# A decoder layer in float32: block B22 loaded by the slot of its first sum, transposes ordered behind the matmuls in front of them

## The chip, the cores and the metric

One Trainium2 chip, of which the kernel uses one core. A core has TensorE (PE, with the weight load drawn apart as PEld), VectorE (DVE), ScalarE (ACT), GpSimd (POOL) and SyncE (SP), each with an instruction queue of its own, and 16 DMA engines that move data between HBM and on-chip memory (SBUF; matmuls write to PSUM). The metric is the device time of one execution in microseconds.

## The reference

One layer of a hybrid decoder on 256 tokens of width 2048, all in float32:

```python
h = rmsnorm(x, g_mix)
x_r, g_r, q, k, v, gate_r, gate_a = split(h @ w_in)
y_r = (gelu(g_r) * rg_lru(conv1d(x_r), ...)) @ w_rnn_out      # recurrent mixer
y_a = stick_breaking_attention(rmsnorm(q), rmsnorm(k), v) @ w_attn_out
x = x + (sigmoid(gate_r) * y_r + sigmoid(gate_a) * y_a) @ w_o
gate, up = split(rmsnorm(x, g_ffn) @ w_ffn_gu)
x = x + (silu(gate) * up) @ w_ffn_down
x = x + sigmoid(rmsnorm(x, g_ple) @ w_ple_gate) * (p @ w_ple_proj)
```

HBM reads are 405 MB, almost all weights, and nearly all of the work is products of 256 tokens with them.

## The kernel before, in words

**Numbers.** A float32 product is made of three matmuls in a reduced format (fp32r). Each weight block of 128 x 1024 numbers (512 KB) is loaded from HBM, ACT copies it to its high half `whi` (L363), DVE subtracts that to get the low half `wlo` (L364), and `prod` (L633) issues three matmuls: activations' high half with `whi` (L635), with `wlo` (L636), and the low half with `whi` (L637). A matmul of 512 columns is the unit of work.

**Fewer products.** From stage `ro` on, a product is cut in 2 x 2 blocks, and for some inner indices seven block products with sums of blocks take the place of eight. The weight blocks concerned are called 11, 12, 21 and 22; a slot called `T1` uses 11 + 12, `T2` uses that sum + 22, `T3` and `T4` are further ones, and `S1` to `S4` are the same for half blocks. These raw blocks come into tiles of the tag Q (31 of them). DVE adds them on chip (L288, in `summed`; for `T2` it is `add(t, t, r[g("22")])`, which therefore needs the block 22 landed), and some sums are made by POOL's transfers that add while they write (`joins`, L326). All other blocks go to `w` tiles, of which there are four (`W_BUFS`); a `w` tile is free again when DVE has made its `wlo`.

**Slots.** A group (`group`, the name with an index as in gu/2 or dn0/0) runs through a list of slots: `FIRST3`, `EVEN3`, `EVEN4`, `LONG` or `TWELVE`. In `EVEN4`, used by v and most of gu, the middle reads `... A2, B2, 10, "21", "T2", 11, "22", A3, 12 ...`: numbers are plain blocks, A and B the S sums. T2 comes ahead of 22, and 22 is needed from T2's addition on. The stages in order: gtr, the recurrent part, ro, v, attention, ao, wo, gu/0 to gu/3, dn0, gu/4 to gu/7, dn1, gu/8 to gu/10, dn2, pg.

**Order of the loads.** SyncE issues all loads of weights from one queue (L277), in an order written down ahead of time by `dma_order`. A list `t` of modelled times of the chunks gives each load a value `begin`; plain blocks by the use of the block whose buffer they take, raw blocks by `t` six chunks in front of their own slot, less `RAW_AHEAD`. `DMA_ORDER` sorts by `begin`. `dma_to` issues loads in this order, chained by `issue_after`, so a load behind one that waits for its buffer waits too. Splits run four chunks ahead of the matmuls in the program, and sums two more.

**Order of the rest.** A scheduler orders the instructions of each engine by its own modelled times when the kernel is built; `issue_after(x)` binds instructions built inside it to come behind x on the same engine. The engines run their queues in order, and semaphores make them wait for one another.

**Transposes.** Activations for the next stage are turned by TensorE against an identity (`next_mix` L1117, `turned` in `next_h` L1165, `turn` in `gu` L1226) and evacuated from PSUM by ACT (L449) and DVE (L443, L446). Such functions are put on the list `pend`; `group` takes one at the slots named in `TURNED_AT` (the fifth, seventh, ninth and eleventh in `FIRST3`, else the ninth to fifteenth). Element work goes on `todo` and is taken from the second slot on.

Of the kernel before, what the change touches and what calls it, by code (L numbers as in the profile page):

```python
# [42 lines left out]
FOUR = ("gu", "v")  # L43
LAST_GROUP = ("pg", 1)
W_BUFS = 4
RAW_AHEAD = 9.0
SUMS_AHEAD = 2
TURNED_AT = {True: (5, 7, 9, 11), False: (9, 11, 13, 15)}
NEG = -1e30
# [2 lines left out]
def pairs_of(name):  # L52

    if name[:2] == "dn":
        q = int(name[2])
        return [FQ0[q] // 2 + i for i in range(3 if FQ[q] == 16 else 2)]
    return (0, 1, 2, 3) if name in FOUR else (0, 1, 2)


def is_sum(x):  # L60

    return isinstance(x, str) or isinstance(x, tuple) and x[0] == "S"


def products(x, two=TWO):


    if isinstance(x, int):
        return [("2", (x, 0), None, 0), ("4", (x, 1), None, 0), ("3", (x, 0), None, 1), ("8", (x, 1), None, 1)]
    bank = {"11": "B", "T1": "5", "T2": "B", "T3": "B", "21": "2", "22": "3", "T4": "4"}  # L70
    if isinstance(x, str):
        return [(bank[x], x, p, c) for c, p in enumerate(two)]
    k = {1: ("11", "21"), 2: ("T1", "T2"), 3: ("22", "T3"), 4: ("T4",)}[x[1]]
    return [(bank[y], y, x[2], c) for c, y in enumerate(k)]
# [118 lines left out]
PLAN = plan()  # L193
# [9 lines left out]
CHUNKS = []  # L203
# [9 lines left out]
    LAST.append(len(CHUNKS))  # L213


def dma_order():


    t, took = [0.0], []
    for i, a, b in CHUNKS:  # L220
        k = PLAN[i][0]
        t.append(t[-1] + (0.68 * len(products(k[3])) if k[0] == "tok" and is_sum(k[3]) else 0.34 * (b - a)))
    plain, begin = [], {}
    for j, (i, _, _) in enumerate(CHUNKS):
        k = PLAN[i][0]
        if k[0] == "tok" and is_sum(k[3]):
            begin[j] = t[max(0, j - 6)] - RAW_AHEAD
        else:
            begin[j] = t[max(0, plain[-W_BUFS] - 4)] if len(plain) >= W_BUFS else 0.0
            plain.append(j)  # L230
    order = sorted(range(len(CHUNKS)), key=lambda j: begin[j])
    at = {j: n for n, j in enumerate(order)}
    upto, m = [0], 0
    for j in range(len(CHUNKS)):
        m = max(m, at[j] + 1)
        upto.append(m)
    return order, upto


DMA_ORDER, DMA_UPTO = dma_order()  # L240
HALVES = (1, 3)
CHUNK_OF = {PLAN[c[0]][0][1:]: j for j, c in enumerate(CHUNKS) if PLAN[c[0]][0][0] == "tok"}


class Stream:
# [37 lines left out]
    def summed(self, key):  # L283
# [33 lines left out]
        t = r[g("R")]  # L317
        self.dma_to(CHUNK_OF[g("22")] + 1)
        add(t, t, r[g("22")])
        return t, 1024  # L320

    def joins(self, t, c, key, a):

        j = CHUNK_OF[key]
        src = self.w[OFFS[j]:OFFS[j] + P * 1024].rearrange("(p c) -> p c", p=P)
# [90 lines left out]
def tile_hybrid_block(ctx: ExitStack, tc: tile.TileContext, xT: bass.AP, x: bass.AP, pT: bass.AP,  # L416
                      prm: bass.AP, w: bass.AP, out: bass.AP):
    nc = tc.nc
# [10 lines left out]
    def tl(tag, dt=F32):  # L429
        cnt[0] += 1  # L430
        tag = "H" if tag in "CT" else "Q"
        n, c = NT[tag]
        return act.tile([P, c], dt, tag=tag, name=f"{tag}_{cnt[0]}", bufs=n)

    def psum():
        cnt[0] += 1
        return pps.tile([P, 512], F32, tag="ps", name=f"ps_{cnt[0]}")
# [4 lines left out]
    def tt(o, a, b, op):  # L442
        nc.vector.tensor_tensor(o, a, b, op)  # L443
# [4 lines left out]
    def actv(o, i, f, **kw):  # L448
        nc.scalar.activation(o, i, f, **kw)  # L449
# [177 lines left out]
    pend, todo = [], []  # L627

    def tok(pairs, k, t):
        x = rhs(pairs, k)  # L630
        return x[:, t * P:t * P + P], x[:, 256 + t * P:384 + t * P]

    def prod(ps, x, wh, wl, start=False, stop=False, goes_on=False):  # L633

        nc.tensor.matmul(ps, x[0], wh, start=start, stop=False, skip_group_check=goes_on)  # L635
        nc.tensor.matmul(ps, x[0], wl, start=False, stop=False, skip_group_check=goes_on)  # L636
        nc.tensor.matmul(ps, x[1], wh, start=False, stop=stop, skip_group_check=goes_on)  # L637

    def half_sums(h):

# [58 lines left out]
    def group(at, pairs, sums, after=None, also=()):  # L699

        name, g = at
        slots = [x for n, y, _, _, _, sl in HEAD + TAIL if (n, y) == at for x in sl
                 if isinstance(x, int) or is_sum(x)]
        seq = [(n, q, 0, 512) for n, x in enumerate(slots) for q in products(x, pairs_of(name)[:2])]
        if at == LAST_GROUP:  # L710
            k = len(slots) - 4
            rest = [q for q in seq if q[0] >= k]
            seq = [q for q in seq if q[0] < k] + [q for b in "243" for q in rest if q[1][0] == b]
            seq += [(n, (b + f, *q), e, e + 256) for e, f in ((0, "a"), (256, "b")) for n, (b, *q), _, _ in rest
                    if b == "8"]
        first, last = {}, {}
        for i, (_, (b, y, _, _), e, _) in enumerate(seq):
            first.setdefault(b, i)
            last[b, e] = i
            if y in ("11", "T1", "T2", "T3"):  # L720
                last[y] = i
        banks, tile_, got = {}, {}, {}
        for i, (n, (b, y, p, c), e0, e1) in enumerate(seq):
            if n not in got:
                if n in also:
                    also[n]()
                if n and todo:
                    todo.pop(0)()
                elif n in TURNED_AT[slots[2] == 6 and slots[8] == "22"] and pend:
                    pend.pop(0)()  # L730
                got[n] = S_.take(("tok", name, g, slots[n]))
            if b not in banks:
                banks[b] = psum()
            ps = banks[b]
            if p is None:
                o = tok(pairs, *y)
            else:
                o = {"11": tok(pairs, 2 * p, 0), "21": tok(pairs, 2 * p + 1, 0), "22": sums[p][3],
                     "T1": sums[p][0], "T2": sums[p][1], "T3": sums[p][2],
                     "T4": tok(pairs, 2 * p + 1, 1)}[y]  # L740
            _, _, hi, lo, w0 = got[n].columns(c)
            s = slice(w0 + e0, w0 + e1)
            prod(ps[:, e0:e1], o, hi[:, s], lo[:, s], i == first[b], i in (last[b, e0], last.get(y)),
                 b == "B")
            if y in ("11", "T1", "T2", "T3") and i == last[y]:
                t = tile_[y] = tl("T")
                actv(t, ps, AF.Copy)
                if y == "T3":
                    tt(tile_["T2"], tile_["T1"], tile_["T2"], ALU.subtract)
                    tt(tile_["T1"], tile_["T1"], t, ALU.subtract)  # L750
                    if after is not None:
                        after(tile_)
        tile_["ends"] = [banks[b] for b in ("8a", "8b") if b in banks]
        return [banks[b] for b in "2438"], tile_


    xc, xcs, gel, y, gtr, ysum, xsum = {}, {}, {}, [], [], {}, {}
# [118 lines left out]
    for i in range(NPD):  # L876
        also.setdefault(2 * i + 1 if i < 7 else 14, []).append(squares_x(i))
    also = {n: (lambda fs: lambda: [f() for f in fs])(fs) for n, fs in also.items()}
    pss = group(("gtr", 0), xg, None, None, also)[0]
    qg = cst.tile([P, 1], F32, tag="qg", name="qg")  # L880
    nc.vector.tensor_scalar(qg, pc(PC_QG, 0), 1.0 / math.sqrt(HD), None, ALU.mult)
# [37 lines left out]
    def whole(at, pairs, sums, also=()):  # L919

        (q2, q4, q3, q8), t = group(at, pairs, sums, None, also)
        cs = [t[y] for y in ("11", "T3", "T2", "T1")]
        for c, q in zip(cs, (q2, q4, q3, q8)):
            tt(c, q, c, ALU.add)
        return cs
# [16 lines left out]
    for g in range(2):  # L942
        also = {n - 4 + i: (lambda p: lambda: parts_sums(xg, xsum, p))(p) for i, p in enumerate(pairs_of("v"))} if g else {
            8: last_gate, 12: next_table}
        for i, c in enumerate(whole(("ro", g), y, ysum, also)):
            o = gtr[2 * g + i // 2][i % 2]
# [240 lines left out]
    for g in range(2):  # L1187
        for b in (2 * g, 2 * g + 1):
            for t in range(2):
                x1[t][b] = tl("C")  # L1190
                nc.sync.dma_start(x1[t][b], x[t * P:t * P + P, b * 512:b * 512 + 512])

        for n, ps in enumerate(group(("wo", g), mix, msum, onto_x1(g))[0]):
            t, b = n % 2, 2 * g + n // 2
            tt(x1[t][b], ps, x1[t][b], ALU.add)
            squares(0, t, b)
        for p in range(4 * g, 4 * g + 4):
            pend.append(next_h(hg, hsum, p, PC_GF))
# [71 lines left out]
    for g in range(2):  # L1270
        qs_, t_ = group(("pg", g), h3, sum3, also={len(FIRST3) - 4: embedded(g)})
        for n, (q, c) in enumerate(zip(qs_, ("11", "T3", "T2", "T1"))):
            t, b, op = n % 2, 2 * g + n // 2, ALU.add
            c, ps, o = t_[c], pp.pop(0), tl("T")
# [3 lines left out]
            for i in range(0, 512, 256 if ends else 512):  # L1278
                s = slice(i, i + 256 if ends else i + 512)
# [71 lines left out]
```

## Time and profile before

| what | us |
|---|---|
| median of 3 runs | 1876.23 |
| lowest and highest | 1874.94, 1877.95 |
| profiled execution | 1876.19 |
| its span, first to last instruction | 1874.2 |
| TensorE busy in the span | 1852.7 |
| VectorE busy | 1501.9 |
| ScalarE busy | 1244.8 |
| GpSimd busy | 115.5 |
| mean granted clock of TensorE | 0.999 |

A line of the timeline gives the start and the length in us, engine, line, operation, the tiles written and read, and how many like it follow one another; in brackets stands the idle time of that engine just before, and what ended it. A row of the waits says which engine and line waited for which, us in total, how many times, and the longest. In a row of windows stand the stretch, its length, the busy times of PE, PEld, DVE, ACT and POOL with counts, the granted clock, the share of DMA and GB/s. "SPq" is SyncE issuing a transfer. Matmuls overlap: each is drawn longer than the distance to the next.

### The profile page before, as it was taken

The page shows a single profiled execution, that of the slowest core. Times are in us where ns is not written, and L with a number is a line of the kernel's source. Part 1 is how long each engine was busy: PE and PEld are TensorE (multiplying, and loading weights), DVE is VectorE, ACT ScalarE, POOL GpSimd, SP SyncE. Part 2 cuts the span into 40 slices and gives each one's busy share as a digit, 9 for nine tenths or more (in the row PEclk, how much of TensorE's full clock was granted, in tenths as well). Part 3 has the DMA queues.
Part 4 walks back from the last instruction along what each step waited for, and adds up shares of the span by engine and source line. Part 5 has one row for each costly group of instructions (what it writes and reads, how often), then busy time and mean ns, then how long its engine had stood idle before and what let it go on. Part 6 is the DMA issues. An engine that isn't in the chain of part 4 may idle for free.

```text
span 1874.2 us, 24711 instructions
## 1 busy us (share of the span) xinstructions
PE 1852.7 (99%) x8885; PEld 1552.3 (83%) x8885; DVE 1501.9 (80%) x1896; ACT 1244.8 (66%) x1670; POOL 115.5 (6%) x140
## 2 busy tenths in 40 slices
PE   9999999999999999999999999999999999999998
PEld 7899989888888888888878787878888778888887
DVE  7688887677887576667798888898788988889986
ACT  6687888765565566777566766665566665666774
POOL 0000000000010000000001011100111101110100
PEclk9999999999999999999999999999999999999999
DMA  8556556677786555556778687878888778888774
GB/s 288 178 178 188 194 182 192 205 225 233 250 251 197 191 158 164 162 158 228 220 232 264 208 254 229 238 222 255 264 254 238 234 237 251 232 232 250 220 236 140
DMA packets 121082, 409.11 MB, mean 218 GB/s; under 512 B 13568, under 2 KB 14208, under 8 KB 120960
## 3 DMA queue, kind: packets, MB, share of 16 engines
q1 hardware_dynamic: 101808, 359.82, 55.3%
q0 software_dynamic: 19008, 47.72, 15.3%
q8 instruction: 69, 1.13, 0.2%
q14 instruction: 53, 0.43, 0.1%
q10 hardware_dynamic: 144, 0.01, 0.0%
HBM read 405.40 MB, written 2.10 MB: 217 GB/s over the span
## 4 chain that ended last, share of the span: by engine, by line
PE 87%; DVE 6%; DMA 3%; issue 2%; ACT 2%; SPq 0%; DVEq 0%; ACTq 0%
PE ps L636 23%; PE ps L637 23%; PE ps L635 23%; PE ps L565 9%; PE ps L569 4%; DVE wlo L364 3%; DMA Q<-in_w_dram 2%; DVE H L443 1%; PE ps L549 1%; PE ps L548 1%; PE ps L547 1%; ACT whi L363 1%; DVE Q L288 1%; DMA w<-in_w_dram 1%; DVE Q L443 1%
## 5 line engine op out<-in xcount | busy, mean ns | idle before, releaser
L636 PE MATMUL ps<-wlo,Q 128*128 128x512 f32 x2185 | 853.9, 391 | 8.3 <-DVE wlo L364 8.3
L637 PE MATMUL ps<-whi,Q 128*128 128x512 f32 x2185 | 849.0, 389 | 0.0
L635 PE MATMUL ps<-whi,Q 128*128 128x512 f32 x2185 | 762.1, 391 | 3.8 <-ACT whi L363 3.2
L364 DVE TENSOR_TENSOR wlo<-w,whi 128x1024 fp32r<-128x1024 f32 (+2 forms) x497 | 598.3, 1210 | 197.1 <-ACT whi L363 193.6
L363 ACT ACTIVATE whi<-w 128x1024 fp32r<-128x1024 f32 (+2 forms) x497 | 518.2, 1048 | 244.8 <-PE ps L637 193.1
L636 PEld LDWEIGHTS ps<-wlo,Q 128*128 128x128 f32 x2185 | 410.6, 188 | 98.0 <-DVE wlo L364 14.4
L635 PEld LDWEIGHTS ps<-whi,Q 128*128 128x128 f32 x2185 | 409.6, 188 | 91.3 <-ACT whi L363 6.8
L637 PEld LDWEIGHTS ps<-whi,Q 128*128 128x128 f32 x2185 | 410.7, 188 | 84.0
L363 ACT ACTIVATE whi<-Q 128x1024 fp32r<-128x1024 f32 (+1 forms) x339 | 338.0, 1005 | 212.6 <-PE ps L637 139.1
L364 DVE TENSOR_TENSOR wlo<-Q,whi 128x1024 fp32r<-128x1024 f32 (+1 forms) x339 | 388.0, 1156 | 56.1 <-ACT whi L363 55.1
L326 POOL DMA_DIRECT2D Q<-in_w_dram x132 | 113.1, 864 | 1710.5 <-DVE Q L288 578.7
L565 PE MATMUL ps<-Q,whi 128*128 128x512 f32 x704 | 170.7, 391 | 0.0
L288 DVE TENSOR_TENSOR Q<-Q,Q 128x512 f32<-128x512 f32 (+1 forms) x132 | 116.2, 888 | 48.2 <-DMA Q<-in_w_dram 47.8
L565 PEld LDWEIGHTS ps<-Q,whi 128*128 128x128 f32 x704 | 128.7, 188 | 24.5
L449 ACT ACTIVATE H<-ps 128x512 f32<-128x512 f32 (+1 forms) x163 | 84.4, 534 | 65.8 <-PE ps L637 54.7
L443 DVE TENSOR_TENSOR H<-H,H 128x512 f32<-128x512 f32 (+1 forms) x208 | 116.9, 572 | 4.3 <-ACT H L449 3.5
L443 DVE TENSOR_TENSOR H<-ps,H 128x512 f32<-128x512 f32 (+1 forms) x154 | 87.4, 603 | 13.7 <-PE ps L637 8.4
L569 PEld LDWEIGHTS ps<-Q,wlo 128*128 128x128 f32 x704 | 90.4, 191 | 3.5
L569 PE MATMUL ps<-Q,wlo 128*128 128x256 f32 x704 | 91.5, 283 | 0.0
L449 ACT ACT_TABLE_LOAD x53 | 68.0, 1283 | 1.6 <-DVE Q L443 0.7
L449 ACT ACTIVATE Q<-H 128x512 fp32r<-128x512 f32 x61 | 37.6, 626 | 33.0 <-DVE H L443 32.2
L443 DVE TENSOR_TENSOR Q<-H,Q 128x512 fp32r<-128x512 f32 (+1 forms) x69 | 47.0, 684 | 0.1
(122 smaller groups left out, 903.8 us busy)
## 6 DMA issues: line engine op xcount, KB each, us to landing
w<-in_w_dram SPq DMA_DIRECT2D x473, 512.0 KB, 4.2
Q<-in_w_dram SPq DMA_DIRECT2D x182, 512.0 KB, 6.1
Q<-in_w_dram POOLq DMA_DIRECT2D x50, 512.0 KB, 6.1
Q<-in_w_dram POOLq DMA_DIRECT2D x82, 256.0 KB, 5.5
w<-in_w_dram SPq DMA_DIRECT2D x16, 448.0 KB, 3.2
H<-in_x_dram SPq DMA_DIRECT2D x8, 256.0 KB, 7.6
H<-in_xT_dram SPq DMA_DIRECT2D x7, 256.0 KB, 5.7
out_dram<-H SPq DMA_DIRECT2D x7, 256.0 KB, 2.9
```

The lines of the kernel that those rows point to most:

```text
L288: add = lambda o, a, b: self.nc.vector.tensor_tensor(o, a, b, ALU.add)
L326: self.nc.gpsimd.dma_start(t[:, c:], src[:, a:a + 1024 - c], accum_op=ALU.add)
L363: self.hi_ins = self.nc.scalar.activation(h, t[:, :c], AF.Copy)
L364: self.lo_ins = self.nc.vector.tensor_tensor(l, t[:, :c], h.bitcast(F32), ALU.subtract)
L443: nc.vector.tensor_tensor(o, a, b, op)
L449: nc.scalar.activation(o, i, f, **kw)
L547: nc.tensor.matmul(o, wt[0], xh, start=start, stop=False)
L565: nc.tensor.matmul(pss[e], wt[0], rhs(xs, k), start=(k == 0), stop=(k == n - 1))
L569: nc.tensor.matmul(pss[e][:, :256], wt[1], rhs(xs, k)[:, :256], start=False, stop=False)
L635: nc.tensor.matmul(ps, x[0], wh, start=start, stop=False, skip_group_check=goes_on)
L636: nc.tensor.matmul(ps, x[0], wl, start=False, stop=False, skip_group_check=goes_on)
L637: nc.tensor.matmul(ps, x[1], wh, start=False, stop=stop, skip_group_check=goes_on)
```

## The change

Three edits. `RAW_AHEAD` goes from 9 to 12, so that raw blocks get smaller values of `begin`. A block 22 gets its value from the slot of `T2` in its group where that comes sooner than its own; `CHUNK_OF` is defined earlier for that. And `prod` returns its last matmul, behind which `group` now binds a function taken from `pend`: its transposes come on TensorE after the last matmul issued in the slots in front. How many instructions there are on each engine stays the same.

```diff
-RAW_AHEAD = 9.0
+RAW_AHEAD = 12.0
...
+CHUNK_OF = {PLAN[c[0]][0][1:]: j for j, c in enumerate(CHUNKS) if PLAN[c[0]][0][0] == "tok"}
...
         if k[0] == "tok" and is_sum(k[3]):
-            begin[j] = t[max(0, j - 6)] - RAW_AHEAD
+            first = min(j, CHUNK_OF[(*k[1:3], "T2")]) if k[3] == "22" else j
+            begin[j] = t[max(0, first - 6)] - RAW_AHEAD
...
     def prod(ps, x, wh, wl, start=False, stop=False, goes_on=False):
...
-        nc.tensor.matmul(ps, x[1], wh, start=False, stop=stop, skip_group_check=goes_on)
+        return nc.tensor.matmul(ps, x[1], wh, start=False, stop=stop, skip_group_check=goes_on)
...
                 elif n in TURNED_AT[slots[2] == 6 and slots[8] == "22"] and pend:
-                    pend.pop(0)()
+                    with tc.issue_after(mm_.ins):
+                        pend.pop(0)()
...
-            prod(ps[:, e0:e1], o, hi[:, s], lo[:, s], i == first[b], i in (last[b, e0], last.get(y)),
+            mm_ = prod(ps[:, e0:e1], o, hi[:, s], lo[:, s], i == first[b], i in (last[b, e0], last.get(y)),
```

More of the change, by code (lines that the diff above doesn't have):

```diff
@@ L241 @@
 HALVES = (1, 3)
-CHUNK_OF = {PLAN[c[0]][0][1:]: j for j, c in enumerate(CHUNKS) if PLAN[c[0]][0][0] == "tok"}
 class Stream:
```

## The prediction

> **What bounds the kernel now.** I read the page's busy times first, then the view of waits, then the timeline around each place where TensorE waited long. The page and the waits:
>
> ```profile
> PE 1852.7 (99%) x8885; PEld 1552.3 (83%) x8885; DVE 1501.9 (80%) x1896; ACT 1244.8 (66%) x1670; POOL 115.5 (6%) x140
> ```
>
> ```profile
> DVE Q L288 <- DMA Q<-in_w_dram: 47.8, 29, 3.9
> ACT whi L363 <- DMA w<-in_w_dram: 19.8, 17, 2.3
> PEld ps L636 <- DVE wlo L364: 14.4, 16, 2.1
> ACT Q L449 <- PE ps L1226: 14.4, 10, 3.0
> PE ps L636 <- DVE wlo L364: 8.3, 12, 1.7
> ```
>
> PE is busy for 1852.7 of 1874.2 us. An order cannot shorten matmuls, so the ceiling of any gain is near the other 21.5 us. The waits say what fills part of it: matmuls wait for their low halves wlo, made by DVE from the high halves whi, which ACT makes. DVE itself waited 47.8 us in 29 places, in its addition at L288, for a raw block still under way. Most of these 29 were covered by splits made ahead; the timeline shows which were not.
>
> Where nothing is late, 512-column matmuls start 0.23 us apart, while each is drawn 0.39 us long:
>
> ```profile
> 1002.25 0.39 PE L637 MATMUL ps<-whi,Q 128*128 128x512 f32 x1
> 1002.48 0.39 PE L635 MATMUL ps<-whi,Q 128*128 128x512 f32 x1
> ```
>
> So a stall costs the idle time shown plus 0.16 (0.39 less 0.23); a matmul drawn 0.50 long after a stall costs 0.11 more. I count such a stall as idle + 0.27.
>
> **Block 22 by the slot of T2.** One complete instance, group gu/2: SyncE's loads, then the addition that makes T2, and what follows.
>
> ```profile
> 1145.22 0.33 SPq L277 DMA_DIRECT2D w<-in_w_dram  x1
> ...
> 1150.36 0.33 SPq L277 DMA_DIRECT2D w<-in_w_dram  x1
> 1150.74 0.47 SPq L277 DMA_DIRECT2D Q<-in_w_dram  x1
> 1157.36 0.33 SPq L277 DMA_DIRECT2D w<-in_w_dram  x1
> 1157.74 0.45 SPq L277 DMA_DIRECT2D Q<-in_w_dram  x1
> ```
>
> ```profile
> 1165.71 1.22 DVE L288 TENSOR_TENSOR Q<-Q,Q 128x1024 f32<-128x1024 f32 x1 [3.54 <-DMA Q<-in_w_dram]
> ...
> 1168.13 0.19 PEld L636 LDWEIGHTS ps<-wlo,Q 128*128 128x128 f32 x1 [2.12 <-DVE wlo L364]
> 1168.13 0.50 PE L636 MATMUL ps<-wlo,Q 128*128 128x512 f32 x1 [1.70 <-DVE wlo L364]
> ```
>
> The last SyncE row is block 22. Raw loads have free buffers; they are late because they stand behind a w load in SyncE's queue, which waits until DVE frees one of four w buffers (each Q load goes out 0.4 us behind a w load). Block 22 lands about 8 us after 1157.74, and DVE stands still for 3.54 us in front of the subtraction for plain slot 10, whose data are long there. TensorE then loses 1.70 + 0.27 = 1.97 us. In the new order of loads, 22 goes out behind block 21 and both pass ahead of the w loads of 1150.36 and 1157.36: the queue is then free from the w load of 1145.22, so 22 is issued at about 1146, 11.7 us sooner. Even with the same 8 us it lands near 1154, ahead of the 1162.2 (1165.71 less 3.54) at which DVE was ready. The other places of this kind, in v/1, gu/5, gu/6, gu/7, gu/9 and gu/10:
>
> ```profile
> 562.04 0.50 PE L636 MATMUL ps<-wlo,Q 128*128 128x512 f32 x1 [1.16 <-DVE wlo L364]
> ```
>
> ```profile
> 1380.53 0.50 PE L636 MATMUL ps<-wlo,Q 128*128 128x512 f32 x1 [0.65 <-DVE wlo L364]
> ```
>
> ```profile
> 1423.20 0.50 PE L636 MATMUL ps<-wlo,Q 128*128 128x512 f32 x1 [0.65 <-DVE wlo L364]
> ```
>
> ```profile
> 1465.24 0.19 PEld L636 LDWEIGHTS ps<-wlo,Q 128*128 128x128 f32 x1 [0.44 <-DVE wlo L364]
> ```
>
> ```profile
> 1636.15 0.50 PE L636 MATMUL ps<-wlo,Q 128*128 128x512 f32 x1 [0.86 <-DVE wlo L364]
> ```
>
> ```profile
> 1679.13 0.50 PE L636 MATMUL ps<-wlo,Q 128*128 128x512 f32 x1 [0.92 <-DVE wlo L364]
> ```
>
> With 0.27 each: 1.43, 0.92, 0.92, 1.13, 1.19; gu/7 has only the weight load's 0.44, which in gu/2 is 0.42 above the matmul's, so 0.02 + 0.27 = 0.29. With gu/2's 1.97 the sum is 7.85 us. Bounds: all of it (7.85) if 22 comes in time; about none, if it is late for another reason. I take all: 11.7 us of lead against waits of at most 3.9. What is late next: DVE comes to wlo of slot 10 some 2 us sooner than TensorE, by its own row durations, and I find no stall behind it.
>
> **RAW_AHEAD 12.** Other raw blocks move one or two places forward in SyncE's queue, past w loads that wait for buffers. Each issue takes 0.45 us of SyncE at most, while SyncE idles for 5 us and more between pairs: cost nil. The loads passed do not move, since their buffers free as before. POOL's 132 accumulating transfers keep their order and their count: nil. Bounds: 0 to the few tenths by which w loads land later beside one more transfer (rival one).
>
> **Transposes held.** Instruction counts stay. In 17 groups four to sixteen transposes move 10 to 67 matmuls back on PE, 2 to 15 us. An order edge is no wait at run time; the costs are what ACT and DVE, first in first out, now meet. Three starts of groups where the transposes themselves stalled PE:
>
> wo/0, transposes waiting on DVE, and then the splits behind them:
>
> ```profile
> 980.20 0.88 PE L1117 MATMUL ps<-ident,Q 128*128 128x128 f32 x6 [0.23 <-DVE Q L443]
> ...
> 981.69 1.20 PE L635 MATMUL ps<-whi,Q 128*128 128x512 f32 x4 [0.15 <-ACT whi L363]
> ...
> 983.67 0.50 PE L636 MATMUL ps<-wlo,Q 128*128 128x512 f32 x1 [0.78 <-DVE wlo L364]
> ```
>
> That is 0.39 + 0.42 + 1.05 = 1.9 us. In the new order twelve of these transposes come 10 to 26 matmuls later, and DVE makes T2's sum and its low half sooner: I take 1.9 as gained; bounds 0 and 1.9.
>
> gu/0, where DVE's addition for T2 stood behind the evacuation of transposes though its block was there:
>
> ```profile
> 1073.36 1.04 PE L1165 MATMUL ps<-ident,H 128*128 128x128 f32 x8
> 1073.60 1.22 DVE L288 TENSOR_TENSOR Q<-Q,Q 128x1024 f32<-128x1024 f32 x1
> ...
> 1075.95 0.50 PE L635 MATMUL ps<-whi,Q 128*128 128x512 f32 x1 [1.56 <-ACT whi L363]
> 1076.90 0.50 PE L635 MATMUL ps<-whi,Q 128*128 128x512 f32 x1 [0.45 <-ACT whi L363]
> ```
>
> ```profile
> 1077.20:1080.70 3.50, 3.50 (x9) 2.83 (x9) 3.50 (x5) 3.50 (x6) 0.85 (x1) 0.51 0.43 54
> ```
>
> Lost: 1.83 + 0.72, and then 3.5 us at a granted clock of 0.51, in which 9 matmuls run where 15 go at 0.23: 1.5 us. Together 4.1. In the new order ACT still has two table loads and an evacuation ahead of whi of T2; by their rows I leave 1.0 + 0.7 + 0.5 of stall and no slow clock: gain 1.9. Bounds: 0.3 (clock drops again) and 3.5.
>
> [...]
>
> dn0/0 (and dn1/0, like it):
>
> ```profile
> 1243.09 0.88 PE L1226 MATMUL ps<-ident,H 128*128 128x128 f32 x6 [0.71 <-DVE H L446]
> ```
>
> ```profile
> 1236.00:1250.00 14.00, 12.31 (x54) 8.66 (x53) 14.00 (x19) 9.55 (x13) 2.57 (x3) 1.00 0.56 131
> ```
>
> DVE has no idle moment in these 14 us. Taking the transposes away leaves TensorE waiting for the same low half a little later: 0 gained; bounds -0.5 and +1 each.
>
> pg/0, which loses. Its rows now:
>
> ```profile
> 1774.18 0.50 PE L635 MATMUL ps<-whi,Q 128*128 128x512 f32 x1 [0.29 <-ACT Q L449]
> 1774.55 0.62 ACT L449 ACTIVATE H<-H 128x512 f32<-128x512 f32 x1
> ```
>
> In the new order all four additions of the last dn sums stand ahead of T1's sum on DVE, all four squares of 0.62 ahead of T1's whi on ACT, and two table loads (1.28 each, the page's 68.0 us over 53) ahead of the whi of T2. Following the queues with these durations TensorE finds new stalls of 0.3, 0.9, 0.1 and 1.15 us; it had 0.56 in its first one here and about 0.3 in a later one: 1.6 us lost. Bounds: 0, and -2.5 if the present stalls stay beside the new ones.
>
> **Sum.** 7.85 + 1.9 + 1.9 + 0 - 1.6 = 10.05 us. The profiled execution took 1876.19 us around a span of 1874.2; 1876.2 - 10.0 = 1866.2. The median shown, 1876.23, is the same within 0.04. The bounds of the unknown terms give from 1876.2 - 7.85 - 1.9 - 3.5 - 2 = 1861 to, with the 7.85 kept and the rest at its low ends, 1876.2 - 7.85 - 0.3 + 1 + 2.5 = 1872.
>
> **Rivals.** *One: raw loads bunch and other loads come late.* In gu/2 a w load, 21 and 22 would go out within 1 us. Block 22 now waits for bandwidth with them, and the w block of 1150.36 lands later. For it: the transfer of 22 took 8 us already. Against it: ACT's waits for w are 19.8 us in 17, and ACT is 66% busy, DVE had 3.5 us to spare. If half of the 7.85 comes back as waits on w, with the rest of the sum kept: 1870. [...]
>
> *Two: nothing comes of it.* Either the stalls at slot 10 have DVE's order as their cause, and 22's landing only ends last; then TensorE waits at slot 10 as long, and the 1.9 of wo/0 and of gu/0 go against pg/0: 2.2 us gained, 1874. For it: DVE is 80% busy, and a gapless DVE in dn0/0 shows what a saturated queue does. Against it: 3.54 us of idle DVE right in front of that subtraction.
>
> *Three: slower.* Held transposes bring their evacuations into the slots in which DVE and ACT make T2 and 22: ACT, first in first out, stands at an evacuation until the transposes run, with whi of the next slots behind it. ACT's present waits for L1226 are 14.4 us in 10, 1.44 each, off the path. If they come onto it in each of the 17 groups: 24 us lost, less 10 gained: 1890. It decides from 0.6 us a group. For it: pg/0, where I find 1.6. Against it: in gu/2, by the row durations, splits stay ahead of TensorE, and there the transposes run in the slot before which they are held, not later than their consumers need.
>
> **How the numbers follow.** Forecast 0.55 (1862 to 1870 by itself); rival one 0.20 (1868 to 1873); rival two 0.12 (1873 to 1878); rival three 0.13 (1880 and more, up to 1890). No change is within 0.2% or 3.75 us, about what a measurement of this kernel tells apart: below 1872.5 is faster, above 1880 slower. Faster is the forecast and nearly all of rival one: 0.74; same 0.13; slower 0.13. The range from 1861 to 1875 leaves out rival three and part of rival two.
>
> **What would show it.** Right: DVE's waits at L288 for Q fall from 47.8 us to under 25, and the seven stalls at slot 10 and in v/1 are gone from the timeline, 22 being issued next to 21; no clock spell in gu/0; wo/0 without stall in its first 15 us; dn0/0 with about 3 us of stalls as before; pg/0 with longer ones. Wrong: more ACT waits for w (rival one), the same slot-10 stalls behind a DVE without idle time (two), or many new waits of ACT at L449 for L1226 and of PE for whi (three).

## The result and the profile after

The changed kernel takes 1867.5 us (median of 5, 1867.4 to 1868.85) where the kernel before takes 1877.95 in the runs beside it (median of 5, 1874.94 to 1882.81). The ratio is 0.9941, with a 95% interval of 0.9922 to 0.9961: faster, inside the stated range and 1.3 us above the predicted 1866.2. By the profiled executions, which the sum was made against, it is 1867.5 to 1876.19; the spans are 1865.5 and 1874.2, 8.7 us apart, where the sum said 10.05. Lines stand three to four further down in the changed file: L288 is now L291, L363 and L364 are L366 and L367, L635 to L637 are L638 to L640, L1226 is L1230.

The chain that ended last, by engine, of the kernel before and then of the changed one:

```profile
PE 87%; DVE 6%; DMA 3%; issue 2%; ACT 2%; SPq 0%; DVEq 0%; ACTq 0%
```

```profile
PE 94%; DVE 3%; ACT 1%; issue 1%; DMA 0%; SPq 0%; ACTq 0%; DVEq 0%
```

Loads have left the chain, and DVE's share is halved. The waits of the changed kernel, in the same columns as before:

```profile
DVE Q L291 <- DMA Q<-in_w_dram: 8.3, 8, 2.1
...
ACT whi L366 <- DMA w<-in_w_dram: 14.4, 15, 2.8
PEld ps L638 <- ACT whi L366: 10.2, 14, 1.5
PEld ps L639 <- DVE wlo L367: 6.1, 3, 2.5
PE ps L638 <- ACT whi L366: 5.0, 10, 1.0
PE ps L639 <- DVE wlo L367: 4.9, 3, 2.1
```

DVE's wait for raw blocks fell from 47.8 us to 8.3, and ACT's for w from 19.8 to 14.4: no other load came late in their place. TensorE's waits for wlo are down from 12 places to 3. Its waits for whi went up, from 3.2 to 5.0 us. In gu/2, SyncE and then DVE:

```profile
1140.48 0.33 SPq L280 DMA_DIRECT2D w<-in_w_dram  x1
1140.86 0.90 SPq L280 DMA_DIRECT2D Q<-in_w_dram  x2
...
1155.57 1.23 DVE L291 TENSOR_TENSOR Q<-Q,Q 128x1024 f32<-128x1024 f32 x1
```

The two Q loads are 21 and 22, one behind the other and directly behind the w load that they stand with in the order; the addition for T2 no longer waits. The three places that were expected to keep or get stalls, gu/0, dn0/0 and pg/0:

```profile
1066.42 1.20 PE L638 MATMUL ps<-whi,Q 128*128 128x512 f32 x4 [0.21 <-ACT whi L366]
...
1071.35 0.51 PE L638 MATMUL ps<-whi,Q 128*128 128x512 f32 x1 [0.52 <-ACT whi L366]
1072.29 0.50 PE L638 MATMUL ps<-whi,Q 128*128 128x512 f32 x1 [0.44 <-ACT whi L366]
```

```profile
1237.53 0.50 PE L639 MATMUL ps<-wlo,Q 128*128 128x512 f32 x1 [2.07 <-DVE wlo L367]
```

```profile
1767.79 0.50 PE L638 MATMUL ps<-whi,Q 128*128 128x512 f32 x1 [1.04 <-ACT whi L366]
...
1772.81 0.50 PE L638 MATMUL ps<-whi,Q 128*128 128x512 f32 x1 [0.90 <-ACT whi L366]
```

The clock does not drop in gu/0: it is 1.00 from 1063 to 1077. Where TensorE loses time, group by group, is the best single account of this change. I worked the table out from the timelines of TensorE: for each matmul or transpose, the distance between two starts beyond 0.227 us for 512 columns, 0.120 for 256 and 0.110 for 128, summed where it is over 0.04 us (slow clock included, in us). The kernels of the experiments stand beside it: the edits of the loads alone (e1), the slot of T2 alone (e2), RAW_AHEAD alone (e3), the hold alone (e4), and the T2 slot with one more edit (e9). Stretches at half clock (granted 0.51 over 1077.20 to 1080.70 in the kernel before, 0.57 over 1691.40 to 1694.90 in e4), 3.41 us long and worth 1.5 to 1.7 us each in this sum, are in three columns: before and e3 have one in gu/0, e4 has one each in wo/0, dn0/0, dn1/0 and gu/10.

| group | before | changed | e1 loads | e2 T2 slot | e3 ahead | e4 hold | e9 |
|---|---|---|---|---|---|---|---|
| v/1 | 1.4 | 0.0 | 0.8 | 0.0 | 0.5 | 3.7 | 0.0 |
| wo/0 | 2.2 | 0.4 | 0.3 | 0.5 | 0.4 | 4.0 | 0.5 |
| gu/0 | 4.3 | 2.5 | 1.0 | 1.6 | 4.2 | 1.1 | 1.6 |
| gu/2, 5, 6, 7, 9, 10 | 7.5 | 1.2 | 0.6 | 1.2 | 0.6 | 14.5 | 1.5 |
| gu/3 | 0.2 | 0.2 | 0.1 | 0.2 | 0.1 | 2.1 | 0.2 |
| dn0/0 and dn1/0 | 6.5 | 7.2 | 6.4 | 6.5 | 6.4 | 8.8 | 4.6 |
| dn0/1 and dn1/1 | 0.0 | 0.0 | 0.0 | 0.0 | 0.0 | 1.7 | 0.0 |
| pg/0 | 1.2 | 3.2 | 3.2 | 2.3 | 2.2 | 3.1 | 1.3 |
| the rest | 8.1 | 8.2 | 8.1 | 7.8 | 8.1 | 8.1 | 8.1 |
| sum | 31.4 | 22.9 | 20.5 | 20.1 | 22.5 | 47.1 | 17.8 |

### The profile page after: what moved, and what is told of

Same layout as the page of the kernel before. It is cut to its first block, busy times and chain, and to the rows that moved or that the text cites. A ratio compares the mean times of both kernels' runs of the same rounds, so it can differ in the third digit from the quotient of the medians.

```text
span 1865.5 us, 24702 instructions
## 1 busy us (share of the span) xinstructions
PE 1848.0 (99%) x8885; PEld 1551.7 (83%) x8885; DVE 1504.6 (81%) x1896; ACT 1250.0 (67%) x1670; POOL 115.6 (6%) x140
## 4 chain that ended last, share of the span: by engine, by line
PE 94%; DVE 3%; ACT 1%; issue 1%; DMA 0%; SPq 0%; ACTq 0%; DVEq 0%
PE ps L640 25%; PE ps L639 25%; PE ps L638 25%; PE ps L568 9%; PE ps L572 5%; PE ps L552 1%; PE ps L551 1%; PE ps L550 1%; DVE wlo L367 1%; DVE H L446 1%; ACT whi L366 1%; PE ps L1230 1%; DVE Q L291 0%; PE ps L997 0%; DMA w<-in_w_dram 0%
## 5 line engine op out<-in xcount | busy, mean ns | idle before, releaser
L640 PE MATMUL ps<-whi,Q 128*128 128x512 f32 x2185 | 848.7, 389 | 0.0
L638 PE MATMUL ps<-whi,Q 128*128 128x512 f32 x2185 | 774.6, 391 | 5.0 <-ACT whi L366 5.0
L367 DVE TENSOR_TENSOR wlo<-w,whi 128x1024 fp32r<-128x1024 f32 (+2 forms) x497 | 599.6, 1212 | 213.6 <-ACT whi L366 208.7
L366 ACT ACTIVATE whi<-w 128x1024 fp32r<-128x1024 f32 (+2 forms) x497 | 518.7, 1049 | 258.3 <-PE ps L640 200.5
L638 PEld LDWEIGHTS ps<-whi,Q 128*128 128x128 f32 x2185 | 409.1, 188 | 92.8 <-ACT whi L366 10.2
L366 ACT ACTIVATE whi<-Q 128x1024 fp32r<-128x1024 f32 (+1 forms) x339 | 339.2, 1006 | 214.0 <-PE ps L640 188.6
L640 PEld LDWEIGHTS ps<-whi,Q 128*128 128x128 f32 x2185 | 410.2, 188 | 84.8 <-DVE Q L446 0.2
L367 DVE TENSOR_TENSOR wlo<-Q,whi 128x1024 fp32r<-128x1024 f32 (+1 forms) x339 | 390.5, 1159 | 67.4 <-ACT whi L366 65.4
L291 DVE TENSOR_TENSOR Q<-Q,Q 128x512 f32<-128x512 f32 (+1 forms) x132 | 115.7, 890 | 8.6 <-DMA Q<-in_w_dram 8.3
```

The costliest lines, as they stand in the source:

```text
L291: add = lambda o, a, b: self.nc.vector.tensor_tensor(o, a, b, ALU.add)
L366: self.hi_ins = self.nc.scalar.activation(h, t[:, :c], AF.Copy)
L367: self.lo_ins = self.nc.vector.tensor_tensor(l, t[:, :c], h.bitcast(F32), ALU.subtract)
L640: return nc.tensor.matmul(ps, x[1], wh, start=False, stop=stop, skip_group_check=goes_on)
```

## Experiments

### The parts alone: e1 to e4

Each starts from the changed kernel. e1 takes the hold away:

```diff
-                    with tc.issue_after(mm_.ins):
-                        pend.pop(0)()
+                    pend.pop(0)()
```

> Both edits of the loads, transposes as before the change. Theory (the prediction's sum): the seven stalls behind block 22 go (7.85 us), those at the starts of wo/0 (1.9 us) and gu/0 (4.1 us) stay, dn0/0 and dn1/0 stay at 3.1 each, pg/0 at 0.9: about 7.9 us faster than before, slightly slower than the whole change (by some 1 us). Rival two (the order on DVE is the cause, not the landing): the stalls at slot 10 stay, under 2 us faster.

e2 takes away the hold and `RAW_AHEAD`:

```diff
-RAW_AHEAD = 12.0
+RAW_AHEAD = 9.0
```

> Only block 22 by the slot of T2, RAW_AHEAD 9, transposes as before. In the order of loads 22 then passes one w load in each of the seven places instead of two. Theory: one is enough; in gu/2 it goes out at about 1151, lands near 1159, and DVE is ready at 1162.2: the whole 7.85 us. Rival: the second w load is needed too (landing after 1162): DVE still waits at L288 for some 1 to 3 us in each place and only about half is gained, 4 us.

e3 takes away the hold and the T2 slot:

```diff
-            first = min(j, CHUNK_OF[(*k[1:3], "T2")]) if k[3] == "22" else j
+            first = j
```

> Only RAW_AHEAD 12, 22 by its own slot, transposes as before. 22 passes one w load here too, other raw blocks one place. Theory: as with the T2 slot alone, 7.85 us, so that each of the two edits of the loads makes the other superfluous. Rival: T2's slot is what matters and earlier issue alone gives under 3 us.

e4 keeps the hold and takes both edits of the loads away:

```diff
-RAW_AHEAD = 12.0
+RAW_AHEAD = 9.0
...
-            first = min(j, CHUNK_OF[(*k[1:3], "T2")]) if k[3] == "22" else j
+            first = j
```

> Only the hold on the transposes, loads in the order of before. Theory: the stalls at slot 10 and in v/1 stay (up to 7.85 us), wo/0 gains 1.9 and gu/0 about 2, dn0/0 and dn1/0 lose 0.4 each, pg/0 loses 1.9: about 1 us faster than before, within the noise. Rival two: the hold clears the stalls at slot 10 by itself, 8 us faster. Rival three: 17 groups with new waits, slower.

Measured on one chip, against the kernel before there (1877.39); the two later sets ran on two other chips:

| kernel | median us | ratio | interval |
|---|---|---|---|
| e1, both edits of the loads | 1864.71 | 0.9936 | 0.9915 to 0.9957 |
| e2, T2 slot alone | 1864.40 | 0.9936 | 0.9914 to 0.9957 |
| e3, RAW_AHEAD alone | 1866.86 | 0.9947 | 0.9930 to 0.9964 |
| e4, hold alone | 1890.74 | 1.0066 | 1.0042 to 1.0091 |

**The loads.** e2 and e3 both clear the gu groups, so one w load passed is enough, and each edit makes the other superfluous there, as expected. The block does not come early everywhere: in gu/2 of e2 DVE still waits for it, as the rival of e2 had it, but TensorE no longer does.

```profile
1156.37 1.22 DVE L291 TENSOR_TENSOR Q<-Q,Q 128x1024 f32<-128x1024 f32 x1 [2.09 <-DMA Q<-in_w_dram]
```

But the sizes are not those expected: e1 and e2 gain about 12 us by their ratios, not 7.9, because wo/0 and part of gu/0 went with the loads, without any hold. (Of gu/0's 4.3 us before, 1.7 are the half-clock stretch; stalls alone went from 2.6 to 1.0 in e1 and 1.6 in e2.) By the list that `dma_order` makes, the T2 slot moves 21 loads, all of them blocks 22, and none of wo/0 or gu/0; yet wo/0 lost 2.2 us before and loses 0.5 in e2. What changed there is the order on the engines: e2 has another instruction than before in 580 of 8885 places of the order on PE and in 285 of 1896 on DVE, and in e1 the transposes of wo/0 come up to 31 matmuls later. The scheduler places everything by modelled times, and with earlier loads it places them elsewhere. These window rows (the stretch, its length, PE, PEld, DVE, ACT, POOL busy, clock, DMA, GB/s) cover the start of wo/0 in the kernel before and in e1:

```profile
972.00:986.00 14.00, 12.84 (x59) 9.80 (x58) 14.00 (x21) 7.19 (x11) 2.10 (x3) 1.00 0.51 136
```

```profile
970.50:984.50 14.00, 14.00 (x67) 11.55 (x66) 14.00 (x19) 7.89 (x10) 1.91 (x3) 1.00 0.62 150
```

DVE has no idle moment in either, and TensorE none in e1: in wo/0 the order of DVE's work was the trouble, and not that DVE had no time left.

**The hold alone is slower, by 0.66%.** Neither sum nor rival two had this; rival three had the sign. The gu groups lose 14.5 us instead of 7.5. In gu/5 of the kernel before, and then of e4:

```profile
1375.62 0.38 PE L1226 MATMUL ps<-ident,H 128*128 128x128 f32 x2
...
1375.76 0.48 PE L636 MATMUL ps<-wlo,Q 128*128 128x512 f32 x1
...
1376.77 0.82 PE L1226 MATMUL ps<-ident,H 128*128 128x128 f32 x6
...
1377.34 1.63 PE L635 MATMUL ps<-whi,Q 128*128 128x512 f32 x6
...
1378.12 1.23 DVE L288 TENSOR_TENSOR Q<-Q,Q 128x1024 f32<-128x1024 f32 x1 [2.09 <-DMA Q<-in_w_dram]
```

```profile
1382.97 1.22 DVE L291 TENSOR_TENSOR Q<-Q,Q 128x1024 f32<-128x1024 f32 x1 [2.29 <-DMA Q<-in_w_dram]
1384.31 1.06 ACT L366 ACTIVATE whi<-Q 128x1024 fp32r<-128x1024 f32 x1 [2.99 <-DVE Q L291]
...
1385.41 0.50 PE L638 MATMUL ps<-whi,Q 128*128 128x512 f32 x1 [2.18 <-ACT whi L366]
```

Before, eight transposes ran ahead of that addition, six of them while DVE waited for block 22: they were TensorE's work in that time. Measured from start to start they took 0.71 us (1375.62 to 1375.76 and 1376.77 to 1377.34). Held behind the matmuls in front, the transposes that belong to later slots wait behind T2's matmuls, which wait for 22. TensorE loses 2.18 + 0.27 = 2.45 us here instead of 0.92: 1.5 more, of which the transposes make about half. DVE's wait for the block is 0.2 us longer (2.29 against 2.09); the rest is not separated here. gu/3, with no stall before, gets 2.1 us; there DVE's wait for 22 grew from 1.47 to 2.58 us, so the hold is not the only cause. In e4 the mean granted clock is 0.995 instead of 0.999: it has the four half-clock spells named above, which the changed kernel's profile does not have.

Not all of e4's 13 us is the hold. The columns of the table are 15.7 us apart (47.1 less 31.4); the spells make some 4.7 of that (6.4 against 1.7) and v/1 makes 2.3. The same load of 22 in v/1, before the first held transpose, in the kernel before and in e4:

```profile
554.09 0.44 SPq L277 DMA_DIRECT2D Q<-in_w_dram  x1
...
559.62 1.23 DVE L288 TENSOR_TENSOR Q<-Q,Q 128x1024 f32<-128x1024 f32 x1 [1.60 <-DMA Q<-in_w_dram]
```

```profile
553.48 0.40 SPq L280 DMA_DIRECT2D Q<-in_w_dram  x1
...
561.34 1.23 DVE L291 TENSOR_TENSOR Q<-Q,Q 128x1024 f32<-128x1024 f32 x1 [3.92 <-DMA Q<-in_w_dram]
```

From issue to use it took 5.5 us in one execution and 7.9 in the other, with the same order of instructions on every engine up to there; v/1 lost 2.3 us more by it. The kernels with late blocks also vary most from run to run: the kernel before ranges over 7.9 us in the five runs beside the result, e4 over 7.6, the changed kernel over 1.5. That the landings make this spread is likely, and not shown run by run.

### What the hold costs, and more lead: e5 to e8

e5 is the changed kernel again. e6 holds only outside dn and pg:

```diff
-                    with tc.issue_after(mm_.ins):
+                    with tc.issue_after(mm_.ins) if name[:2] not in ("dn", "pg") else nullcontext():
```

e7 is e2 with the gating products in front of dn0/0 and dn1/0 moved to ACT and GpSimd; e8 is e1 with `RAW_AHEAD = 20.0`. The edit of e7:

```diff
+                if g in (3, 7):
+                    actv(s_, s_, AF.Identity, scale=rs1[:, t:t + 1])
+                    nc.gpsimd.tensor_tensor(c, c, s_, ALU.mult)
+                    return
                 stt(c, c, rs1[:, t:t + 1], s_, ALU.mult, ALU.mult)
```

> The changed kernel again, beside the variants of this set on one chip. Theory after the first set: the whole change equals the edits of the loads plus a small cost of the hold, so about 9 us faster than before, and 2 to 3 us slower than the edits of the loads alone were (0.9936). Rival: no difference between them but that of the chips.

> The whole change, but transposes are not held in the groups of dn and pg. Theory: what the hold costs lies in dn0/0, dn1/0 (0.4 each) and pg/0; with their order as in the loads alone these go back, and gu/0 keeps the hold's 2.1 us of stalls: between the whole change and the loads alone, 0.5 to 1.5 us faster than the whole. Rival: the hold helps wo/0 and gu/0 after all, then this is the fastest, 3 us faster than the whole change.

> Block 22 by T2's slot alone (the fastest so far), and in gu/3 and gu/7 the two products in front of dn0/0 and dn1/0 move from DVE (0.75 us each) to an ACT scaling and a GpSimd multiplication. Theory: DVE without an idle moment is what stalls TensorE by 3 us at dn0/0 and dn1/0; with 1.5 us less on it, 1 to 1.5 us of each go: 2 to 3 us faster than the T2 slot alone, near 0.992 of before. Rival: the transposes wait for GpSimd's slower product instead, the same or slower.

> Edits of the loads without the hold, RAW_AHEAD 20 in place of 12: 22 passes four w loads in the gu groups. Theory: the lead of one w load was enough already, so no stall is left to take away there; raw blocks sit longer in the 31 tiles, and where one is not free SyncE stands, and w loads behind it come late: the same as with 12, or 1 to 3 us slower, ACT's waits for w above 19 us. Rival: still faster, because DVE's remaining waits at L291 (7.5 us in all with 12) go too; at most 1 us, since none of them reaches TensorE.

On a second chip (the kernel before there: 1876.14):

| kernel | median us | ratio | interval |
|---|---|---|---|
| e5, the whole change | 1867.79 | 0.9952 | 0.9938 to 0.9967 |
| e6, no hold in dn and pg | 1866.24 | 0.9945 | 0.9930 to 0.9959 |
| e7, T2 slot, products on GpSimd | 1868.50 | 0.9955 | 0.9938 to 0.9971 |
| e8, loads with a lead of 20 | 1866.61 | 0.9946 | 0.9931 to 0.9961 |

**e6** is 1.6 us faster than e5, but not for the reason expected in full: its dn0/0 and dn1/0 are back at 3.2 each, while pg/0 still loses 3.2, as it does in e1 without any hold. These are other stalls of the same sum. The hold alone (e4, the first two rows) has pg/0's stalls nearly as the changed kernel has them, 1.04 and 0.90; the loads without the hold (e1, the last two) have others:

```profile
1792.51 0.50 PE L638 MATMUL ps<-whi,Q 128*128 128x512 f32 x1 [1.10 <-ACT whi L366]
...
1797.53 0.50 PE L638 MATMUL ps<-whi,Q 128*128 128x512 f32 x1 [0.86 <-ACT whi L366]
```

```profile
1765.35 0.50 PE L638 MATMUL ps<-whi,Q 128*128 128x512 f32 x1 [0.50 <-ACT whi L366]
...
1771.09 0.50 PE L638 MATMUL ps<-whi,Q 128*128 128x512 f32 x1 [1.57 <-ACT whi L366]
```

So either edit by itself costs pg/0 some 2 us, and taking one away leaves the other's loss. gu/0 keeps its 2.5.

**e7** is not faster than e2, against the theory: 1868.50 here, e2 1864.40 on the first chip. Its dn0/0 and dn1/0 lose 4.9 and 4.4 us, against 3.2 and 3.3 in e2; a half-clock spell makes 1.6 of the 4.9. The same slots of e7 and, below, e2:

```profile
1232.09 2.85 POOL L1219 TENSOR_TENSOR H<-H,H 128x512 f32<-128x512 f32 x2
1232.28 3.22 DVE L446 TENSOR_TENSOR Q<-H,Q 128x512 fp32r<-128x512 f32 x1
```

```profile
1231.66 0.69 DVE L446 TENSOR_TENSOR Q<-H,Q 128x512 fp32r<-128x512 f32 x1
```

While GpSimd multiplies two tensors, one DVE instruction of 0.69 us takes 3.22. DVE loses more (2.5 us) than it was relieved of (1.4). This run cannot decide whether DVE's load stalls dn0/0.

**e8** gains nothing over 12, as the theory said (1866.61; e1 1864.71 on the first chip), and its ACT waits for w are 19.7 us against e1's 18.5. What it shows besides: wo/0 has its stalls back, 0.28 and 0.37 and 0.28 us of idle TensorE at 980.87, 984.73 and 985.90, with all loads in time. gu/0 loses only 0.4 us there. Each lead gives the scheduler another order, and these places come out well or badly with it.

### The order at dn0/0: e9 to e11

e9 (on the T2 slot alone) and e10 (on the whole change) take no work from DVE; they order the two gating products behind a low half made ahead:

```diff
                 if n and todo:
-                    todo.pop(0)()
+                    with tc.issue_after(S_.lo_ins.ins) if name[:2] == "dn" else nullcontext():
+                        todo.pop(0)()
```

> Block 22 by T2's slot alone, and in the groups of dn the two gating products of 0.7 us, on DVE, are ordered behind the low half of the last block split so far instead of in front of T1's. Theory: it is the place of these products in DVE's queue that stalls TensorE at dn0/0 and dn1/0 (3.1 us each with the T2 slot alone); DVE makes T1's low half 1.4 us sooner, and 1.4 to 3 us of each go: 3 to 5 us faster than the T2 slot alone. Rival: DVE without an idle moment over 14 us only moves the wait to the next block, the same time.

> The whole change with the same order edge on the gating products in the groups of dn. Theory: the 2.2 us stall for T1's low half and what follows it at dn0/0 and dn1/0 (3.4 us each in the changed kernel) shrink by 1.4 to 3 us each: 3 to 5 us faster than the whole change. Rival: the same time as the whole change.

> Block 22 by T2's slot alone, once more, as the base for the run beside it on the same chip. All theories: about 0.9936 of before; against the whole change 2 to 3 us faster, if the hold costs what the traces add up to, and no different from it if the chips made that difference.

On a third chip (the kernel before there: 1878.17):

| kernel | median us | ratio | interval |
|---|---|---|---|
| e9, T2 slot, gating products later | 1861.48 | 0.9915 | 0.9901 to 0.9928 |
| e10, whole change, gating products later | 1864.47 | 0.9931 | 0.9918 to 0.9945 |
| e11, T2 slot alone | 1864.24 | 0.9930 | 0.9918 to 0.9943 |

e9 is 2.8 us faster than e11 on the same chip, and the fastest kernel of this study; nine tenths of a microsecond of it come from each of dn0/0 and dn1/0 (3.2 to 2.3), and 1.0 from pg/0, whose order changed too. In e2, the same program as e11, and then in e9:

```profile
1234.27 0.44 PE L1229 MATMUL ps<-ident,H 128*128 128x128 f32 x2 [0.28 <-DVE H L449]
1234.93 0.88 PE L1229 MATMUL ps<-ident,H 128*128 128x128 f32 x6 [0.22 <-DVE H L449]
1236.07 0.50 PE L639 MATMUL ps<-wlo,Q 128*128 128x512 f32 x1 [0.26 <-DVE wlo L367]
```

```profile
1233.80 1.22 DVE L367 TENSOR_TENSOR wlo<-Q,whi 128x1024 fp32r<-128x1024 f32 x1
...
1235.08 0.50 PE L639 MATMUL ps<-wlo,Q 128*128 128x512 f32 x1 [0.74 <-DVE wlo L367]
```

T1's low half stands in front of the products now, and no transpose waits for them; 0.74 us of idle is left at one wait, where e2 has 0.28, 0.22 and 0.26 at three. The expected 1.4 to 3 us a place was too much: TensorE comes to that low half sooner too, with no transposes in front of it, and the two waits behind it, for the high halves of the next blocks, stay. e10 on the whole change gives 2.6 us a place instead of 3.6. That e9 beats e10 by 3.0 us on one chip is what hold and larger lead cost together when both have the late products; in e10 gu/0 has 2.5 us of stalls and pg/0 3.1, against 1.6 and 1.3 in e9.

## Why the prediction was right

**The sum held; of the reasons for its smaller terms, one was wrong and one was only half of it.** (The ceiling of 21.5 us was too low: busy time counts drawn-out matmuls (0.50 us after a stall, 0.39 else) and slow ones, PE's fell from 1852.7 to 1848.0 us, and the table finds 31.4 us lost.)

*The stalls behind block 22* were the right cause, with the right size: 7.85 us were forecast, and v/1 and the six gu groups went from 8.9 to 1.2 us, 7.7 us. e2 and e3 show that the place in SyncE's queue does it, with one w load passed.

*wo/0* gained 1.8, where 1.9 was forecast, but the step "transposes held" gave it the wrong author. e1 and e2 have wo/0 at 0.3 and 0.5 us without the hold, and e4, the hold without the loads, has it at 4.0, of which 1.6 are a spell. The edits of the loads were costed as a move in SyncE's queue alone; that they make the scheduler order the other engines anew was left out, and it is what the 1.8 us here come from. That the size fits is luck.

*gu/0* gained 1.8, where 1.9 was forecast, and nearly all of it is the clock, as the sum had it: the spell of the kernel before (1.7 us) did not come, and the stalls went from 2.6 to 2.5 us, where 2.2 was forecast. Either part alone does better, 1.0 us (e1) and 1.1 (e4), so neither is the one author. With both, the two table loads (1.28 us each) and two evacuations (0.58 and 0.46) stand ahead of T2's whi on ACT, as the queue walk had it. Whether the kernel before has this spell in every execution is not known; one profile of it is on record.

*dn0/0 and dn1/0*: 0 forecast, 0.7 lost in the two together. The low half of T1 comes as late as before and the transposes, which filled 0.9 us, come later still.

*pg/0*: 1.6 us forecast as lost, 2.0 lost; the walk through the queues found the places and their sizes (1.04 and 0.90 us of idle). The hold does bring these two (e4 has them, 1.10 and 0.86), as forecast; what the forecast did not have is that the order which the loads bring costs as much without the hold (e1: 3.2).

*"An order edge is no wait at run time"*: true where wo/0 of the changed kernel shows it (TensorE is busy for 14.00 of the 14.00 us from 970.50 on, held transposes among its work), and not the whole price. The cover that such an edge moves away was not named. With 22 late the hold comes out 13 us slower than before (e4, spells and slow landings being a part of it); with 22 in time it costs about 2.4 us (22.9 against 20.5 in the table).

**The rivals.** One did not come: ACT waited less for w. Two is out by e2 and e3. Three was the right worry about the wrong resource: ACT does not stand at evacuations (its waits for these transposes, 14.4 us before, are gone in the changed kernel and in e4); TensorE stands without its transposes. In these runs that decided where 22 was late.

**The clock.** No spell came in gu/0, as taken. Whether one comes is not settled by the stalls in front of it. The same stretch of dn0/0, with the same stalls, in the changed kernel and in its second profile, e5:

```profile
1239.50:1242.50 3.00, 2.78 (x12) 1.94 (x12) 3.00 (x3) 3.00 (x4) 0.87 (x1) 1.00 0.11 5
```

```profile
1239.50:1242.50 3.00, 3.00 (x9) 2.09 (x9) 3.00 (x4) 3.00 (x4) 0.87 (x1) 0.56 0.05 7
```

One runs at 1.00 of the clock and one at 0.56. In the kernel before, the clock changes at 1077.26, 1080.68 and 1872.57 us, 1 and 232 times 3.413 us apart; in e4 two of the spells begin at 985.32 and 1691.88, 207 times 3.413 us apart. Counted off in this step from the changes in each trace, the 3.413 us in front of e5's spell, from 1235.29 on, hold the starts of five matmuls, and those of the changed kernel with the same stall, from 1233.90 on, six. Nor was TensorE idle all through such a stretch where a spell followed: in front of the one in the kernel before, from 1073.85 on, it holds three matmuls and three transposes, and in front of e4's at 1691.88, from 1688.47 on, five matmuls.

That the clock would not drop in gu/0, 1.5 of the 1.9 us forecast there, was the author's estimate, and no run shows a reason for it. What the runs showed is where a spell came. The one in dn0/0 of e5 came with no transposes around it. At dn0/0 and dn1/0 of the kernel before, e1, e2 and e6, six such stretches hold four or five matmuls and eight transposes (in the kernel before those from 1241.10 and 1497.10 on), and none was followed by a spell; all four stretches with five matmuls and no transpose (three in e4, one in e5) were, and so were those in gu/0 of the kernel before and of e3, with three or four matmuls and three or five transposes. So beside three to five matmuls, eight transposes went with a clock that stayed, and five or fewer with one that dropped; why was not shown. In gu/0 of the changed kernel no stretch of 3.413 us holds fewer than seven matmuls, and there the clock stayed at 1.00.

## What to carry to other kernels

A transfer that is late for an engine's queue is best looked for in the queue of the loads: what stands in front of it there, and what that waits for. Work held back by an order edge may be the cover of somebody's wait; before holding it, say what the engine does in that time instead. Where a scheduler orders every engine by modelled times, an edit of one queue is an edit of all of them, so each part has to be run alone before a gain is put to its name. Here one third of the change, the slot of T2, is as fast as both edits of the loads on the same chip (1864.40 and 1864.71) and very likely faster than the whole: the slot and the whole were run twice each but on different chips, and their ranges lie apart, 1863.56 to 1866.24 and 1866.99 to 1868.85.

## What the runs showed of the hardware that was not expected

While GpSimd ran two multiplications of two tensors (2.85 us in e7), the DVE instruction Q<-H,Q of 128x512 took 3.22 us; in e2, with no multiplication beside it, it took 0.69. What made it longer was not shown. And the same 512 KB load took 5.5 us from issue to use in one execution (the kernel before, v/1) and 7.9 in another (e4) with no difference in the order ahead of it. It is seen in one program too: in v/1 of e2 and of e11 blocks 21 and 22 go out at 547.15 and 547.11, and T2's addition starts at 558.01 without a wait and at 559.29 after one of 1.25 us. How much of the 8 us over which the kernel before and e4 spread comes from this was not measured.
